# Reordering the detoured half of an exact attention: scores, fetches and GpSimd cuts of the long sequence

## The chip, the cores and the metric

The kernel runs on one core of one Trainium2 chip. The metric is the device time of one execution in microseconds (us), as a median over runs. Each core has TensorE (PE; its weight loads are shown as PEld), VectorE (DVE), ScalarE (ACT), GpSimd (POOL) and SyncE (SP), which here only issues DMAs. Each engine works through its own list of instructions in order, and they wait for each other with semaphores.

## The reference

One encoder layer over two sequences, x_prompt with 1024 tokens and x_sample with 512, width 1024, all in float32. Branch A is grouped-query attention: 8 query heads, 2 key/value groups of 4 heads each, head size 64, normalised and rotated q and k.

```python
def block(qi):
    s = jnp.einsum('bqkgd,bskd->bkgqs', qi, k, preferred_element_type=jnp.float32) * scale
    p = jax.nn.softmax(s, axis=-1)
    return jnp.einsum('bkgqs,bskd->bqkgd', p.astype(v.dtype), v)
...
merged = jax.nn.sigmoid(ga) * (o_a @ w_proj_a) + jax.nn.sigmoid(gb) * (o_b @ w_proj_b)
return merged @ w_out
...
h = h + _token_mixer(_rmsnorm(h, norm_mix_g[l]), ...)
hn = _rmsnorm(h, norm_mlp_g[l])
h = h + jnp.square(jax.nn.relu(hn @ w_mlp_up[l])) @ w_mlp_down[l]
```

Branch B (neighbourhood attention), the gates and the two-layer MLP are computed as well; the change does not touch them.

## The kernel before

Matrix products keep float32 precision by splitting each operand into a high part (rounded to fp32r by ScalarE) and a low part (value minus high part, by VectorE or GpSimd), and multiplying the parts separately. The kernel takes the short sequence first, then the long one, then the MLP. For each sequence and each of the two groups g there is a projection stage and then an attention stage, phase `phA`. In the profile the attention stages of the long sequence (NB == 2) lie at about 445 to 575 us (g = 0) and 640 to 765 us (g = 1).

An attention stage of the long sequence has eight units (h, qb): head h of the group, 512 queries (qb = 0 or 1), 1024 keys. A unit's scores are four tiles of 128 queries, one `step_s(u, j)` each:

- `s_tile` (L801 to L814): four score matmuls into a PSUM tile ss of 1024 columns (there are two such tiles); VectorE takes the maximum (nms, L804); ScalarE takes the exponential into an SBUF tile ps (L811; there are eight such buffers, tag "P"); VectorE takes the reciprocal of the sum (rls, L813); GpSimd multiplies by it (L814).
- For qb = 1, `turn_a` (L856, L857) follows at the next `step_s`: VectorE transposes the tile in blocks of 32 x 32 and SyncE writes it to DRAM (tas).

The value product needs the probabilities with keys on partitions. The two halves get there differently.

- *Transposed unit*, qb = 0: `t_chunk` (L838 to L842) transposes a chunk of 128 keys on TensorE (pTs); ScalarE makes the high part pths, VectorE the low part ptls.
- *Detoured unit*, qb = 1: `fetch_a` (L882) reads a quarter back from DRAM, 512 KB with the block order changed, into hqs. The first three quarters take slots of a shared pool of eleven; three are to be had, so a fetch for the next head needs the slot of the same quarter of this one to have been read. The fourth quarter takes two of the eight ps buffers. `cut_a` splits a quarter: ScalarE writes the high part (L887), GpSimd subtracts in place (L888, one instruction of 128x1024).

`pv` (L825, L826) multiplies a chunk's high and low part with the values, two matmuls into os; `next_pv` runs two chunks behind. A chunk of a detoured unit reads half of each of a quarter's 16 blocks of 64 columns: `(t[:, :, kc % 2 * 32 : kc % 2 * 32 + 32] for t in quarter[...])`. Between these, `fill.pull` puts matmuls of branch A's gate (gpss, L214), whose weights are loaded and split too (w_gs, L201 on ScalarE and L208 on VectorE).

After the first eight score tiles, of (0,1) and (0,0), each head h runs two loops of eight steps kc: in the first the transposed unit's chunks are transposed, in the second the detoured unit's chunks are queued. The order in which this is written is a priority: a planner at build time writes each engine's list by it and by its own estimate of when operands and buffers are ready, so neighbouring pieces can change places.

Of the kernel before, what the change touches and what calls it, by code (L numbers as in the profile page):

```python
# [11 lines left out]
F32 = mybir.dt.float32  # L12
# [3 lines left out]
ALU = mybir.AluOpType  # L16
# [45 lines left out]
def encoder(ctx: ExitStack, tc: tile.TileContext, xs, outs, w):  # L62
    nc = tc.nc
# [359 lines left out]
    def run(tr, nxt, first):  # L423
# [9 lines left out]
        fill = Fill()  # L433
# [105 lines left out]
        for g in range(2):  # L539
            with phase(f"phR{N}_{g}") as ph:  # L540
# [175 lines left out]
                for tt in range(NT):  # L716
# [19 lines left out]
                    op = nc.sync.dma_start(rt, w["rope"][tt * P : (tt + 1) * P])  # L736
# [52 lines left out]
            with phase(f"phA{N}_{g}") as ph:  # L789
# [55 lines left out]
                def next_pv():  # L845
                    if len(queue) > LAG:
                        pv(*queue.pop(0))
# [11 lines left out]
                def step_s(u, j):  # L859
                    end = s_tile(u, j)  # L860
                    while due:
                        turn_a(*due.pop(0))
                    if u[1]:
                        due.append((u, j))
                    return end
# [3 lines left out]
                def fetch_a(u, i):  # L869
                    nm = f"{N}_{g}_{u[0]}_{i}"  # L870
                    if i < 3:
                        hl = slot([P, 2, 16, 64], F32R, f"hq{nm}")
                        hi, lo = hl[:, 0], hl[:, 1]
                    else:
                        hi, lo = (
                            ph.tile([P, T], F32, tag="P", name=f"hq{nm}_{e}", bufs=8)
                            .bitcast(F32R)
                            .rearrange("p (a w) -> p a w", w=64)
                            for e in range(2)
                        )  # L880
                    src = PD[u].rearrange("t (a i) (b w) -> i b (t a) w", i=32, b=4)[:, :, :, 64 * i : 64 * i + 64]
                    nc.sync.dma_start(lo.bitcast(F32), src)  # L882
                    quarter[u, i] = hi, lo

                def cut_a(u, i):
                    hi, lo = quarter[u, i]
                    nc.scalar.activation(hi, lo.bitcast(F32), AF.Copy)  # L887
                    nc.gpsimd.tensor_tensor(lo, lo.bitcast(F32), hi.bitcast(F32), op=ALU.subtract)  # L888

                if NB == 2:  # L890
                    for u in ((0, 1), (0, 0)):
                        for j in range(4):
                            last_exp[:] = [step_s(u, j)]
                            fill.pull(1)
                    for h in range(4):
                        for kc in range(NT):
                            t_chunk((h, 0), kc)
                            if h < 3 and kc in (1, 4):
                                step_s((h + 1, 1), kc // 4)
                            if kc < 4:  # L900
                                fetch_a((h, 1), kc)
                            if 3 <= kc < 6:
                                cut_a((h, 1), kc - 3)
                            fill.pull(1 if kc % 4 < 3 else 0)
                            next_pv()
                        for kc in range(NT):
                            if kc == 1:
                                cut_a((h, 1), 3)
                            if h < 3 and kc < 6:
                                step_s(*(((h + 1, 1), 2 + kc // 3) if kc % 3 == 0 else ((h + 1, 0), kc - 1 - kc // 3)))  # L910
                            hi, lo = (t[:, :, kc % 2 * 32 : kc % 2 * 32 + 32] for t in quarter[(h, 1), kc // 2])
                            queue.append(((h, 1), kc, hi, lo))
                            fill.pull(0 if kc in (2, 5) else 1)
                            next_pv()
                else:
                    for j in range(4):
                        ends = s_tile(units[0], j)
                        last_exp[:] = [ends]
                        fill.pull(2)
                    for ui, u in enumerate(units):  # L920
                        h, qb = u
                        if first:
                            bias_row(g * 4 + ui)
                            if g == 0 and ui == 1:
                                early["a"] = load_a(1)
                            if g == 0 and ui == 2:
                                early["v"] = load_v(1, slot)
                        nxt_u = units[ui + 1] if ui + 1 < len(units) else None
                        sdone = 0
                        for kc in range(NT):  # L930
                            t_chunk(u, kc)
                            if nxt_u is not None:
                                while sdone < 4 and kc >= (0, 0, 1, 2)[sdone]:
                                    s_tile(nxt_u, sdone)
                                    sdone += 1

                            fill.pull(1)
                            next_pv()
# [1146 lines left out]
```

## Time and profile before

| what | value |
|---|---|
| median of 3 runs | 2114.34 us (2113.94 to 2116.36) |
| profiled execution, its own time | 2112.54 us |
| its span, first to last instruction | 2110.7 us |
| TensorE busy | 2072.8 us, 98% |
| VectorE, ScalarE, GpSimd busy | 1491.8, 1143.9, 441.1 us |
| mean granted TensorE clock | 0.999 |

The rows of a timeline give start, length, engine, line, operation, output <- inputs, shape and count; in brackets stands how long the engine stood idle before and what ended that. Rows of a group give busy time and the mean length in ns, then the idle time before them. Rows of a source line give minimum, median and maximum length in ns, then first and last start. Rows of waits give total, number and longest in us.

### The profile page before, as it was taken

How to read it: one execution, taken by the hardware profiler on the slowest of the kernel's cores; microseconds unless marked ns; L12 is line 12 of the kernel's file. 1: busy time of each engine (PE TensorE's matmuls, PEld its weight loads, DVE VectorE, ACT ScalarE, POOL GpSimd, SP SyncE). 2: the span in 40 equal slices, each digit the busy share in tenths (PEclk: the TensorE clock that was granted, in tenths of full speed). 3: DMA queues.
4: the chain of work that ended last, by engine and by line, in shares of the span. 5: the costliest groups of instructions: out<-in, count | busy, mean ns of one | idle time of the engine just before them, and what ended most of it. 6: DMA issues, size and time to landing. Idle time of an engine off the chain costs nothing.

```text
span 2110.7 us, 31228 instructions
## 1 busy us (share of the span) xinstructions
PE 2072.8 (98%) x10615; PEld 1808.7 (86%) x10615; DVE 1491.8 (71%) x2761; ACT 1143.9 (54%) x2455; POOL 441.1 (21%) x478
## 2 busy tenths in 40 slices
PE   9999999999999999999999999999999999999998
PEld 8887878986797778888888999999999988888887
DVE  6665886778658766778864877787777777669563
ACT  6664653766666655556522566565556634334442
POOL 2232310346535634543101100012000000000000
PEclk9999999999999999999999999999999999999999
DMA  6437557556635686776553565478444899688561
GB/s 193 135 103 209 160 162 254 179 134 173 168 82 153 184 197 197 236 237 210 177 197 135 190 200 192 157 242 222 148 156 150 285 346 343 210 277 280 161 209 61
DMA packets 406758, 406.45 MB, mean 193 GB/s; under 512 B 97599, under 2 KB 333767, under 8 KB 406599
## 3 DMA queue, kind: packets, MB, share of 16 engines
q1 hardware_dynamic: 368119, 339.16, 52.3%
q10 hardware_dynamic: 31328, 45.11, 6.4%
q0 software_dynamic: 7152, 20.19, 3.6%
q8 instruction: 84, 1.38, 0.3%
q14 instruction: 75, 0.61, 0.1%
HBM read 291.06 MB, written 114.10 MB: 192 GB/s over the span
## 4 chain that ended last, share of the span: by engine, by line
PE 69%; POOL 4%; issue 2%; DVE 2%; DMA 1%; ACT 1%; ACTq 0%; POOLq 0%; SPq 0%; DVEq 0%
PE dn L214 20%; PE ua L214 6%; PE ud L214 6%; PE uc L214 6%; PE gpss L214 5%; PE ops L214 4%; PE ub L214 3%; PE ppbs L214 2%; PE ppas L214 2%; PE pqbs L214 2%; PE pkbs L214 2%; PE zs L214 2%; POOL ps L814 2%; POOL hqs L888 2%; PE zvs L214 2%
## 5 line engine op out<-in xcount | busy, mean ns | idle before, releaser
L214 PE MATMUL dn<-wd,ah 128*128 128x512 f32 x1248 | 384.3, 389 | 0.0
L214 PEld LDWEIGHTS dn<-wd,ah 128*128 128x128 f32 x1248 | 234.2, 188 | 48.6
L214 PE MATMUL dn<-wd,al 128*128 128x512 f32 x624 | 242.8, 389 | 0.0
L1559 ACT ACTIVATE ah<-ar 128x512 fp32r<-128x512 f32 x168 | 104.0, 627 | 198.1 <-PE dn L214 184.9
L214 PE MATMUL gpss<-xs_0h,w_gs 128*128 128x512 f32 x512 | 185.8, 400 | 0.4 <-DVE w_gs L208 0.3
L1560 DVE TENSOR_TENSOR al<-ar,ah 128x512 fp32r<-128x512 f32 x168 | 113.9, 686 | 72.8 <-ACT ah L1559 63.0
L214 PE MATMUL ud<-B,A 128*128 128x384 f32 x768 | 143.6, 334 | 0.7 <-DVE c L1677 0.7
L214 PE MATMUL uc<-B,A 128*128 128x384 f32 x768 | 143.7, 334 | 0.0
L214 PE MATMUL ua<-B,A 128*128 128x384 f32 x768 | 138.8, 334 | 0.0
L214 PEld LDWEIGHTS dn<-wd,al 128*128 128x128 f32 x624 | 117.1, 188 | 24.4
L214 PEld LDWEIGHTS ud<-B,A 128*128 128x128 f32 x768 | 134.0, 188 | 1.1 <-DVE c L1677 1.1
L214 PEld LDWEIGHTS uc<-B,A 128*128 128x128 f32 x768 | 134.0, 188 | 0.2 <-ACT A L1559 0.2
L214 PEld LDWEIGHTS ua<-B,A 128*128 128x128 f32 x768 | 133.7, 188 | 0.2
L811 ACT ACTIVATE ps<-ss,nms 128x1024 f32<-128x1024 f32 (+1 forms) x96 | 93.5, 975 | 65.5 <-DVE nms L804 53.3
L180 POOL TENSOR_TENSOR rs_f<-ms_f,mhalf 128x1 f32<-128x1 f32 x6 | 4.0, 668 | 590.7 <-DVE ms_f L176 590.7
L814 POOL TENSOR_SCALAR ps<-ps,rls 128x1024 f32<-128x1024 f32 (+1 forms) x96 | 95.7, 999 | 129.9 <-DVE rls L813 113.9
L804 DVE TENSOR_REDUCE nms<-ss 128x1 f32<-128x1024 f32 (+1 forms) x96 | 99.3, 1037 | 30.1 <-PE ss L802 28.9
L214 PE MATMUL ops<-wh_os,mgs 128*128 128x512 f32 x384 | 119.5, 390 | 0.0
L214 PEld LDWEIGHTS gpss<-xs_0h,w_gs 128*128 128x128 f32 x512 | 96.1, 189 | 18.8 <-DVE w_gs L208 0.7
L214 PE MATMUL gpss<-xs_0l,w_gs 128*128 128x512 f32 x256 | 101.3, 396 | 0.0
L1559 ACT ACTIVATE A<-S 128x512 fp32r<-128x512 f32 x128 | 75.8, 623 | 31.5 <-DVE S L1622 22.7
L214 PE MATMUL gpss<-xs_1h,w_gs 128*128 128x512 f32 x256 | 90.2, 394 | 0.0
(299 smaller groups left out, 5169.8 us busy)
## 6 DMA issues: line engine op xcount, KB each, us to landing
ar<-ud SPq DMA_DIRECT2D x120, 512.0 KB, 4.7
br<-in_w_mlp_down_dram SPq DMA_DIRECT2D x72, 512.0 KB, 4.9
rawu<-in_w_mlp_up_dram SPq DMA_DIRECT2D x64, 512.0 KB, 4.1
ud<-c ACTq DMA_DIRECT2D x128, 192.0 KB, 3.3
raw_gs<-in_w_in_dram SPq DMA_DIRECT2D x32, 512.0 KB, 3.9
tas<-ps SPq DMA_DIRECT2D x32, 512.0 KB, 2.8
hqs<-tas SPq DMA_DIRECT2D x32, 512.0 KB, 7.0
ud<-cs SPq DMA_DIRECT2D x64, 192.0 KB
```

The source lines that it names most:

```text
L180: op = nc.gpsimd.tensor_tensor(r[:, :n], m[:, :n], mhalf[:, :n], op=ALU.pow)
L214: op = nc.tensor.matmul(out, a, b, **kw)
L804: nc.vector.tensor_reduce(nm_, s, axis=AX.X, op=ALU.max, negate=True)
L811: op = nc.scalar.activation(to, of, AF.Exp, bias=nm_, accum_out=l)
L814: nc.gpsimd.tensor_scalar(p, p, rl, 1.0, op0=ALU.mult, op1=ALU.mult)
L888: nc.gpsimd.tensor_tensor(lo, lo.bitcast(F32), hi.bitcast(F32), op=ALU.subtract)
L1559: nc.scalar.activation(hi, src, AF.Copy)
L1560: nc.vector.tensor_tensor(lo, src, hi.bitcast(F32), op=ALU.subtract)
```

## The change

Only branch A of the long sequence is touched.

- The subtract of `cut_a` becomes two instructions, over blocks 0 to 7 and 8 to 15.
- The first three fetches of unit (0,1) stand ahead of the first head's loops. For later heads, quarters 0 and 1 are fetched in steps 4 and 6 of the second loop of the head before, quarter 2 in step 0 and quarter 3 in step 2 of the head's own first loop. (Before: quarters 0 to 3 in steps 0 to 3.)
- The cuts stand in steps 1, 2 and 5 of the first loop and step 0 of the second. (Before: 3, 4, 5 and 1.)
- Detoured scores: all four tiles of (1,1) stand in the first head's first loop; those of (h+2,1) are spread over steps 5 and 7 of head h's second loop and steps 1 and 4 of head h+1's first loop. (Before: (h+1,1) in steps 1 and 4 of head h's first loop and steps 0 and 3 of its second.)
- Transposed scores of (h+1,0) stand in steps 0, 1, 2 and 4 of the second loop (before: 1, 2, 4 and 5). In the second loop the steps that pull no gate matmuls are 1 and 4 (before: 2 and 5).

```diff
                 def cut_a(u, i):
                     hi, lo = quarter[u, i]
                     nc.scalar.activation(hi, lo.bitcast(F32), AF.Copy)
-                    nc.gpsimd.tensor_tensor(lo, lo.bitcast(F32), hi.bitcast(F32), op=ALU.subtract)
+                    for a in (slice(0, 8), slice(8, 16)):
+                        nc.gpsimd.tensor_tensor(lo[:, a], lo[:, a].bitcast(F32), hi[:, a].bitcast(F32), op=ALU.subtract)
...
+                    for i in range(3):
+                        fetch_a((0, 1), i)
                     for h in range(4):
+                        u, nn, nd = (h, 1), (h + 1, 0), (h + 1, 1)
                         for kc in range(NT):
                             t_chunk((h, 0), kc)
-                            if h < 3 and kc in (1, 4):
-                                step_s((h + 1, 1), kc // 4)
-                            if kc < 4:
-                                fetch_a((h, 1), kc)
-                            if 3 <= kc < 6:
-                                cut_a((h, 1), kc - 3)
+                            if h == 0 and kc in (0, 2, 4, 6):
+                                step_s(nd, kc // 2)
+                            elif 0 < h < 3 and kc in (1, 4):
+                                step_s(nd, 2 + kc // 4)
+                            if kc == 0 and h > 0:
+                                fetch_a(u, 2)
+                            if kc == 2:
+                                fetch_a(u, 3)
+                            if kc in (1, 2, 5):
+                                cut_a(u, kc // 2)
                             fill.pull(1 if kc % 4 < 3 else 0)
                             next_pv()
                         for kc in range(NT):
-                            if kc == 1:
-                                cut_a((h, 1), 3)
-                            if h < 3 and kc < 6:
-                                step_s(*(((h + 1, 1), 2 + kc // 3) if kc % 3 == 0 else ((h + 1, 0), kc - 1 - kc // 3)))
-                            hi, lo = (t[:, :, kc % 2 * 32 : kc % 2 * 32 + 32] for t in quarter[(h, 1), kc // 2])
-                            queue.append(((h, 1), kc, hi, lo))
-                            fill.pull(0 if kc in (2, 5) else 1)
+                            if kc == 0:
+                                cut_a(u, 3)
+                            if h < 3 and kc in (0, 1, 2, 4):
+                                step_s(nn, min(kc, 3))
+                            if h < 2 and kc in (5, 7):
+                                step_s((h + 2, 1), kc // 7)
+                            hi, lo = (t[:, :, kc % 2 * 32 : kc % 2 * 32 + 32] for t in quarter[u, kc // 2])
+                            queue.append((u, kc, hi, lo))
+                            fill.pull(0 if kc in (1, 4) else 1)
                             next_pv()
+                            if h < 3 and kc in (4, 6):
+                                fetch_a(nd, kc // 2 - 2)
```

## The prediction

> **What bounds the kernel now.** I read, in this order: the page's busy shares, the sums by stage, the waits of TensorE in each stage, and the timelines around the longest waits. "Stage 1" and "stage 2" are the two attention stages of the long sequence, one for each key/value group: the only place that the diff touches.
>
> ```profile
> span 2110.7 us, 31228 instructions
> PE 2072.8 (98%) x10615; PEld 1808.7 (86%) x10615; DVE 1491.8 (71%) x2761; ACT 1143.9 (54%) x2455; POOL 441.1 (21%) x478
> ```
>
> The sums by stage (columns: length, then busy time of PE, PEld, DVE, ACT, POOL, then the granted clock):
>
> ```profile
> 445.00:580.00 135.00, 125.85 (x600) 97.92 (x599) 101.36 (x135) 87.47 (x143) 75.42 (x48) 1.00 0.65 169
> 640.00:775.00 135.00, 125.67 (x594) 97.43 (x593) 98.00 (x135) 84.80 (x134) 74.42 (x49) 1.00 0.69 183
> ```
>
> TensorE is the bound: it idles 2110.7 - 2072.8 = 37.9 us in all, and 135 - 125.85 = 9.15 us in stage 1 and 135 - 125.67 = 9.33 us in stage 2, at a granted clock of 1.00 in both. The diff changes neither the number nor the shape of TensorE's instructions, so its gain lies inside these 18.5 us. The waits of stage 1 (in total, times, longest):
>
> ```profile
> PE os L826 <- POOL hqs L888: 4.0, 4, 1.7
> PE pTs L838 <- POOL ps L814: 2.6, 5, 0.9
> PE os L826 <- DVE ptls L842: 1.2, 2, 0.9
> PE os L825 <- DVE ptls L842: 0.4, 1, 0.4
> ```
>
> And of stage 2:
>
> ```profile
> PE os L826 <- POOL hqs L888: 3.5, 2, 1.8
> PE pTs L838 <- POOL ps L814: 2.6, 5, 0.9
> PE pTs L838 <- DVE ptls L842: 1.7, 1, 1.7
> ```
>
> Three kinds: the value product of a detoured unit waits for GpSimd's subtract of a cut (7.5 us in both stages), the transposes of a transposed unit wait for GpSimd's normalisation (5.2), and both wait for VectorE's low halves ptls (1.2 + 0.4 + 1.7).
>
> **The change, part by part.**
>
> *Fetches and cuts earlier (term 1).* Now all four score tiles of a detoured unit are turned and written before any of its fetches may start, and its last score stands half a head before its first fetch. The last unit of stage 1 shows the consequence (SyncE's four fetches; GpSimd's first cut; TensorE's waits; the row of 755.33 is stage 2's):
>
> ```profile
> 553.34 7.00 SPq L882 DMA_DIRECT2D hqs<-tas  x4
> 560.36 2.37 POOL L888 TENSOR_TENSOR hqs<-hqs 128x1024 fp32r<-128x1024 f32 x1 [8.28 <-ACT hqs L887]
> 562.78 0.50 PE L826 MATMUL os<-hqs,vhls 128*128 128x512 f32 x1 [1.10 <-POOL hqs L888]
> 566.19 0.50 PE L826 MATMUL os<-hqs,vhls 128*128 128x512 f32 x1 [0.33 <-POOL hqs L888]
> 574.38 0.50 PE L826 MATMUL os<-hqs,vhls 128*128 128x512 f32 x1 [0.88 <-POOL hqs L888]
> 755.33 0.50 PE L826 MATMUL os<-hqs,vhls 128*128 128x512 f32 x1 [1.79 <-POOL hqs L888]
> ```
>
> The fetches run from 553.3 to 560.3, the first cut is subtracted at 560.4 after GpSimd stood idle 8.28 us, and TensorE, with nothing else left, waits 1.10 + 0.33 + 0.88 = 2.31 us; stage 2's last unit costs 1.79 us. After the change the last unit's scores end in the first loop of the head before, its first two fetches are issued in that head's second loop as slots are read, the third at the start and the fourth in the third step of its own head. Its data should lie in SBUF some 10 us sooner, against a lateness of 2 us: these 4.1 us go. In the middle of the stage, VectorE first:
>
> ```profile
> 503.92 3.54 DVE L208 TENSOR_TENSOR w_gs<-raw_gs,w_gs 128x512 fp32r<-128x512 f32 x2
> 507.38 0.21 DVE L813 RECIPROCAL rls<-ls 128x1 f32<-128x1 f32 x2
> ```
>
> GpSimd and TensorE beside it, and the same wait in stage 2:
>
> ```profile
> 503.90 2.40 POOL L888 TENSOR_TENSOR hqs<-hqs 128x1024 fp32r<-128x1024 f32 x1 [0.93 <-ACT hqs L887]
> 507.70 2.23 POOL L814 TENSOR_SCALAR ps<-ps,rls 128x1024 f32<-128x1024 f32 x2 [1.40 <-DVE rls L813]
> 509.90 2.35 POOL L888 TENSOR_TENSOR hqs<-hqs 128x1024 fp32r<-128x1024 f32 x1
> 514.59 2.23 POOL L814 TENSOR_SCALAR ps<-ps,rls 128x1024 f32<-128x1024 f32 x2
> 512.30 0.50 PE L826 MATMUL os<-hqs,vhls 128*128 128x512 f32 x1 [1.73 <-POOL hqs L888]
> 515.76 0.33 PE L838 MATMUL pTs<-ident,ps 128*128 128x128 f32 x1 [0.61 <-POOL ps L814]
> 704.22 0.51 PE L826 MATMUL os<-hqs,vhls 128*128 128x512 f32 x1 [1.73 <-POOL hqs L888]
> ```
>
> The third cut (509.90) stands behind two normalisations that wait for VectorE's reciprocal at 507.38, and ends at 512.25, when TensorE has waited 1.73 us; the row of 704.22 is stage 2's, the same 1.73. In the new order the first two cuts stand in the second and third step of the head and the third in the sixth, ahead of the second loop's scores. Sum of the term: 4.1 + 3.46 = 7.56, the 7.5 of the two wait rows. Bounds: 0 (data or cuts are as late as now) and 7.5. I take 7.5, since the fetches move by much more than TensorE waits.
>
> *Next transposed unit's scores first (term 2).* The wait of 0.61 at 515.76 ends with a normalisation that ran only at 514.59, right after the cuts. Its like in the next head:
>
> ```profile
> 544.68 0.33 PE L838 MATMUL pTs<-ident,ps 128*128 128x128 f32 x1 [0.85 <-POOL ps L814]
> ```
>
> Together 1.46, and as the rows of both stages show the same 2.6 in five such waits, 2.9 for both. The third cut now leaves that place, the fourth stays just ahead of these scores: I take half, 1.5, with bounds 0 and 2.9.
>
> *Subtract by halves (term 3).* Of the split's two instructions no matmul can start after one: a value product reads all 16 blocks, and the halves divide these. What changes is how long GpSimd keeps others out. VectorE's subtract of a gate weight took 503.92 to 506.85 beside the cut of 503.90, against 0.67 where it met none:
>
> ```profile
> L208 DVE TENSOR_TENSOR w_gs<-raw_gs,w_gs x4: 669/1483/2934, 472.4 to 506.8; 128x512 fp32r<-128x512 f32 x4
> 473.61 2.29 DVE L208 TENSOR_TENSOR w_gs<-raw_gs,w_gs 128x512 fp32r<-128x512 f32 x1
> 476.62 0.50 PE L826 MATMUL os<-ptls,vhls 128*128 128x512 f32 x1 [0.93 <-DVE ptls L842]
> L368 POOL TENSOR_TENSOR B<-ta,B x12: 1286/1300/1312, 1151.0 to 1437.9; 128x512 fp32r<-128x512 f32 x12
> L888 POOL TENSOR_TENSOR hqs<-hqs x12: 2353/2402/2958, 469.5 to 566.7; 128x1024 fp32r<-128x1024 f32 x12
> ```
>
> Such a block (2.29, where 0.67 is its own) held the ptls that TensorE waited 0.93 us for; stage 2's like is the 1.7. A half should last as a 128x512 subtract of GpSimd does, 1.30: the longest block falls by 2.40 - 1.30 = 1.1, and the two waits from 0.93 + 1.7 to about 0.6. Gain 2.0, bounds 0 (VectorE has to wait for both halves) and 2.6. The price is 2 x 1.30 - 2.40 = 0.2 us a cut, 3.2 us a stage on GpSimd, which has 135 - 75.4 = 59.6 us free: nothing, as long as the cuts are early; if they were still last, 0.2 on each of the six waits, 1.2.
>
> [...]
>
> *First head heavier (term 4, a cost).* All four scores of unit (1,1) now stand in the first head's first loop, two before. One costs VectorE a maximum, a reciprocal and a turn:
>
> ```profile
> L804 DVE TENSOR_REDUCE nms<-ss 128x1 f32<-128x1024 f32 x32 | 38.8, 1213 | 12.6 <-PE ss L802 12.5
> L813 DVE RECIPROCAL rls<-ls 128x1 f32<-128x1 f32 x32 | 4.7, 150 | 2.5 <-ACT ps L811 2.3
> L856 DVE STREAM_TRANSPOSE ps<-ps 128x1024 f32<-128x1024 f32 x16 | 19.7, 1233 | 2.8 <-POOL ps L814 2.7
> 466.00:483.00 17.00, 16.07 (x81) 12.50 (x80) 15.38 (x21) 13.54 (x22) 13.52 (x8) 1.00 0.94 210
> 480.70 1.25 DVE L856 STREAM_TRANSPOSE ps<-ps 128x1024 f32<-128x1024 f32 x1 [0.45 <-POOL ps L814]
> ```
>
> That is 1.21 + 0.15 + 1.23 = 2.6 us, and two of them 5.2. VectorE has 17 - 15.38 = 1.6 free there. But the third turn runs at 480.70 already, so about one comes forward: 2.6 - 1.6 = 1.0 a stage, 2.0 in all; bounds 0 and 10.4. Buffers are short there too: of eight score tiles (0,0) holds four and the fourth fetch, one step earlier than now, two, which leaves two for the four tiles of (1,1); a score without one waits in PSUM, and its price is within the same 10.4.
>
> *Fetches blocked (term 5, a cost).* A fetch into a slot that is still read holds SyncE, and behind it stand turned tiles' writes and gate weights; ScalarE, in order too, stands when it reaches a cut whose data is not there. The 16 fetches a stage stay 7.00 / 4 = 1.75 us of SyncE each. On GpSimd a cut moved forward now stands ahead of normalisations, but they can be placed between its halves, so it holds them 1.30 instead of 2.40.
>
> ```profile
> DMA to landing us min/median/max: 4.2/7.0/8.1
> ACT hqs L887 <- DMA hqs<-tas: 3.0, 5, 1.3
> ```
>
> Stage 2 shows 3.0 us of it on ScalarE, which works 84.8 of 135 us. TensorE has gate matmuls to put in; I take 1.0 in all. Bounds 0 and the price of rival (c).
>
> **Sum.** -7.5 - 1.5 - 2.0 + 2.0 + 1.0 = -8.0 us. The profiled execution took 2112.54 us (span 2110.7 and 1.8 around it), 1.8 under the median 2114.34; it would take 2104.5, and the median 2106.3, -0.38%.
>
> **Rivals.**
>
> (a) The waits only move. The order on each engine is written afresh by the planner, and its misjudged times give new waits of the old size; in the first head VectorE is short by the full 5.2 us a stage. Then 10.4 takes the place of 2.0 in term 4: +0.4, 2114.7; if only the last units' 4.1 go, 2110.2. For it: VectorE's 15.38 of 17. Against it: at the end of a stage no score is left, so the 4.1 have nothing to turn into.
>
> (b) More goes: terms 1 to 3 at their upper bounds and no cost, 7.5 + 2.9 + 3.3 (all ptls waits shown, 1.2 + 0.4 + 1.7) = 13.7, 2100.6.
>
> (c) ScalarE stands at the cuts. Twelve cuts of sixteen stand in first loops, beside the transposes' high halves, and now nearer the head's start; in the first head the first two stand 2 and 3 steps behind their fetches instead of 4. If each of the 24 is reached x us before its data and TensorE pays all of it, the sum is -11 + 2 + 24x; slower than the bound of 0.2% from x = 0.55, about the 3.0 / 5 = 0.6 of the row above. At x = 0.8, within the 8.1 - 7.0 by which the slowest landing exceeds the median, it is +10.2, 2124.5. Against it: a cut is planned where its data is expected, and now 1 of 16 waits in stage 1.
>
> (d) VectorE goes between the halves and the cuts end later: 1.30 + 0.67 + 1.30 = 3.27 for 2.40. If the cuts are still last at the six waits, term 1 is +6 x 0.87 = +5.2 and the sum +4.7, 2119.0. Against it: the earlier fetches of term 1 would have to fail first. [...]
>
> **Chances.** Forecast 0.53, (b) 0.07, (a) 0.27, (c) 0.10, (d) 0.03. Two medians of this kernel under 0.2% (4.2 us) apart can hardly be told from no change. Faster: forecast and (b), 0.60; same: (a), 0.27; slower: (c) and (d), 0.13. The range runs from (b)'s 2100.6, rounded down to 2100, to 2117.0, a little past (a)'s worse value; the forecast alone lies in 2101 to 2110.
>
> **What would show it.** Right: no waits for hqs at the end of either stage, with the last cut well before TensorE's last value product; the L208 subtracts under 2 us; idle time of TensorE in the two stages near 5 us each; everything after stage 2 shifted by 8 us and otherwise alike. Wrong: waits for ptls or for turned scores in the first head (a), ScalarE waiting for hqs landings with the transposed halves behind it (c), or stages before and after these two changing in length, which nothing here provides for.

## The result and the profile after

The changed kernel takes 2105.72 us (median of 7 runs, 2104.78 to 2108.55); the kernel before took 2115.63 us beside it (7 runs, 2113.85 to 2117.34). The ratio is 0.9957, with a 95% interval of 0.9945 to 0.9968: faster by 0.43%. The forecast was 2106.3 us, a ratio of 0.9962 on the median then known.

The profiled execution after took 2105.40 us (span 2103.6), the one before 2112.54 us. So the profiles show 7.1 us of the 9.9 between the medians; the last experiment asks about the rest. The page after, span and busy shares:

```profile
span 2103.6 us, 31314 instructions
PE 2072.8 (99%) x10615; PEld 1809.0 (86%) x10615; DVE 1477.5 (70%) x2761; ACT 1142.2 (54%) x2455; POOL 445.6 (21%) x510
```

TensorE's work is the same 2072.8 us to the tenth; what fell is its idle time, from 37.9 to 2103.6 - 2072.8 = 30.8 us. The sums of the two attention stages (columns as before; each window has moved with the work, and the first ends 5 us sooner because the stage does):

```profile
445.00:575.00 130.00, 124.08 (x593) 96.92 (x592) 98.05 (x137) 87.49 (x147) 78.20 (x64) 1.00 0.68 177
635.00:770.00 135.00, 130.62 (x614) 101.08 (x613) 93.82 (x140) 87.05 (x139) 81.83 (x69) 1.00 0.72 190
```

TensorE now idles 130 - 124.08 = 5.9 us in stage 1 (9.15 before) and 135 - 130.62 = 4.4 us in stage 2 (9.33 before): 10.3 instead of 18.5. TensorE's waits in stage 1 after (total, times, longest):

```profile
PE pTs L838 <- DVE ptls L842: 2.9, 3, 1.4
PE pTs L838 <- POOL ps L814: 1.0, 3, 0.4
PE ss L801 <- ACT ps L811: 0.8, 1, 0.8
PE os L826 <- DVE ptls L842: 0.6, 2, 0.4
```

And in stage 2:

```profile
PE pTs L838 <- DVE ptls L842: 1.5, 2, 0.7
PE pTs L838 <- POOL ps L814: 1.0, 3, 0.4
PE ss L801 <- ACT ps L811: 0.8, 1, 0.8
PE os L826 <- DVE ptls L842: 0.8, 3, 0.4
```

The row that led both lists before, the value product waiting for a cut (hqs), is gone: 7.5 us to nothing. The waits for normalised scores (ps) fell from 2.6 to 1.0 in each stage. The waits for the low halves (ptls) did not fall; they rose from 3.9 us before (the 1.2 + 0.4 + 1.7 shown and 0.4 + 0.2 more in stage 2) to 2.9 + 0.6 + 1.5 + 0.8 = 5.8 us. One instruction behind stage 2 shows the shift of all that follows, first in the timeline before, then in the one after:

```profile
787.82 0.44 PE L214 MATMUL sbs<-kBs,qBs 128*128 128x384 f32 x1 [0.48 <-DVE kBs L1120]
```

```profile
779.80 0.45 PE L214 MATMUL sbs<-kBs,qBs 128*128 128x384 f32 x1 [0.48 <-DVE kBs L1132]
```

It runs 8.02 us sooner with the same wait of 0.48 before it; 0.9 us of that is lost again behind it, where the change doesn't reach (the spans differ by 7.1).

### The profile page after: what moved, and what is told of

Read it like the earlier page. It is cut to its first block, busy times and chain, and to the rows that moved or that the text cites. A ratio compares the mean times of both kernels' runs of the same rounds, so it can differ in the third digit from the quotient of the medians.

```text
span 2103.6 us, 31314 instructions
## 1 busy us (share of the span) xinstructions
PE 2072.8 (99%) x10615; PEld 1809.0 (86%) x10615; DVE 1477.5 (70%) x2761; ACT 1142.2 (54%) x2455; POOL 445.6 (21%) x510
## 3 DMA queue, kind: packets, MB, share of 16 engines
q8 instruction: 84, 1.38, 0.3%
```

## The experiments

Four parts of the change can be taken apart: the subtract by halves, the places of the fetches and cuts, the places of the detoured units' scores (their *lead*), and the transposed units' scores first in their loop. Theory F is the one of the prediction's first term as its heading has it: earlier fetches and cuts removed the hqs waits, and the halves shortened the ptls waits. Theory D says that the lead did it: a fetch can't start before the last turned tile of its unit has been written, so places of fetches mean little without it. A third point is the clock. Each time is told against the kernel before on the same chip.

### The halves alone, and the change without them

On the kernel before:

```diff
-                    nc.gpsimd.tensor_tensor(lo, lo.bitcast(F32), hi.bitcast(F32), op=ALU.subtract)
+                    for a in (slice(0, 8), slice(8, 16)):
+                        nc.gpsimd.tensor_tensor(lo[:, a], lo[:, a].bitcast(F32), hi[:, a].bitcast(F32), op=ALU.subtract)
```

Expected:

> The kernel before with the subtract in two halves and nothing else. TensorE's idle time in the two stages was 18.5 us before and is 10.3 after the whole change. My theory (terms add; halves are term 3): only the two waits behind a blocked VectorE subtract go, idle about 16.5 us, time 2 us under before; the waits for hqs stay near 7.5. [...] Second rival (halves cost, term 1's bound): cuts end 0.2 us later, idle 19 to 20, time 1 us over before. Under both, gate-weight subtracts last at most about 1.5 us where they lasted 2.9.

And the changed kernel with the same lines put back to the whole subtract. Expected:

> The changed kernel with the subtract as one instruction again. My theory: only the blocked VectorE comes back; waits for hqs stay at 0 because the cuts are early; idle 10.3 + 2 = about 12.5, time 2 us over the changed kernel. [...] Second rival (halves are pure overhead once the cuts are early): idle 10, time equal.

Measured: the halves alone 2116.34 us against 2115.67 before, ratio 1.0004 (0.9995 to 1.0013); the change without them 2106.06, ratio 0.9956 (0.9944 to 0.9969), beside the 0.9957 of the whole change. The first kernel's source line of the gate-weight subtract and its waits for cuts and low halves in stage 1 (the cut is line 889 there):

```profile
L208 DVE TENSOR_TENSOR w_gs<-raw_gs,w_gs x4: 680/1482/1815, 474.9 to 508.1; 128x512 fp32r<-128x512 f32 x4
```

```profile
PE os L826 <- POOL hqs L889: 4.7, 5, 1.9
PE os L826 <- DVE ptls L842: 1.1, 2, 0.9
```

The mechanism is there: the longest gate-weight subtract falls from 2934 to 1815 ns, as 1.1 us was predicted. But the ptls wait of 0.9 stays, and the hqs wait grows from 4.0 to 4.7. In stage 2 the ptls wait of 1.7 does shrink, to 0.5; TensorE idles 18.0 us in both stages instead of 18.5, where 16.5 was expected, and no run's time shows it. In this profile a stretch of 3.41 us at half clock (see below) takes half of that, 1.7 us, as well, so the halves alone do not price themselves. The other run tells more: without the halves the changed kernel idles 9.1 us in the two stages where it idles 10.3 with them, and its gate-weight subtracts in stage 1 are just as short (source line of the changed kernel, then of the one with the whole subtract):

```profile
L208 DVE TENSOR_TENSOR w_gs<-raw_gs,w_gs x4: 666/677/1403, 478.0 to 516.9; 128x512 fp32r<-128x512 f32 x4
L208 DVE TENSOR_TENSOR w_gs<-raw_gs,w_gs x4: 665/676/1406, 477.7 to 516.4; 128x512 fp32r<-128x512 f32 x4
```

So the new order shortens them, not the halves. No gain of the halves is seen here, with or without the rest of the change.

### The scores put back, the fetches put back

The changed kernel with both kinds of scores, and the steps that pull no gate matmuls, at their old places (fetches, cuts and halves stay):

```diff
-                            if h == 0 and kc in (0, 2, 4, 6):
-                                step_s(nd, kc // 2)
-                            elif 0 < h < 3 and kc in (1, 4):
-                                step_s(nd, 2 + kc // 4)
+                            if h < 3 and kc in (1, 4):
+                                step_s(nd, kc // 4)
...
-                            if h < 3 and kc in (0, 1, 2, 4):
-                                step_s(nn, min(kc, 3))
-                            if h < 2 and kc in (5, 7):
-                                step_s((h + 2, 1), kc // 7)
+                            if h < 3 and kc < 6:
+                                step_s(*((nd, 2 + kc // 3) if kc % 3 == 0 else (nn, kc - 1 - kc // 3)))
...
-                            fill.pull(0 if kc in (1, 4) else 1)
+                            fill.pull(0 if kc in (2, 5) else 1)
```

Expected:

> The changed kernel with all scores (and the steps without gate matmuls) where they stood before; fetches, cuts and halves stay moved. My theory: a fetch cannot start before its unit's last score tile is turned and written, so the first fetches of a head start only some 2 to 4 us sooner than before instead of some 10, and the last unit's waits for hqs come back in part (2 of 4.1 us); with term 2's 1.5 lost as well, idle about 13.5 to 14, time 3 to 4 us over the changed kernel. Rival (places of fetches and cuts alone do it): no hqs waits, idle about 10 to 11, time equal to the changed kernel.

The changed kernel with fetches and cuts at their old places (scores and halves stay):

```diff
-                    for i in range(3):
-                        fetch_a((0, 1), i)
...
-                            if kc == 0 and h > 0:
-                                fetch_a(u, 2)
-                            if kc == 2:
-                                fetch_a(u, 3)
-                            if kc in (1, 2, 5):
-                                cut_a(u, kc // 2)
+                            if kc < 4:
+                                fetch_a(u, kc)
+                            if 3 <= kc < 6:
+                                cut_a(u, kc - 3)
...
-                            if kc == 0:
+                            if kc == 1:
                                 cut_a(u, 3)
...
-                            if h < 3 and kc in (4, 6):
-                                fetch_a(nd, kc // 2 - 2)
```

Expected:

> The changed kernel with fetches and cuts where they stood before; scores and halves stay moved. My theory: fetches issue at the head's start at once, since the data has long been written, but land about 7 us later and the four cuts take 4 x 2.6 us of GpSimd: at the end of a stage about half of the 4.1 us of hqs waits return, idle about 12.5 to 13, time 2 to 3 us over the changed kernel. Rival (the scores alone do it): no hqs waits, idle about 10 to 11, time equal. Second rival (fetches alone do it): all 7.5 us of hqs waits return, idle 17.

Measured: old scores 2127.67 us, ratio 1.0054 (1.0042 to 1.0067), slower than before; old fetches 2107.18, ratio 0.9963 (0.9949 to 0.9976), nearly the whole gain. Stage 1's waits with old scores, and SyncE's timeline for the last unit there:

```profile
PE pTs L838 <- POOL ps L814: 3.3, 5, 1.1
PE os L826 <- DVE ptls L842: 2.5, 3, 1.3
PE ss L801 <- ACT ps L811: 2.5, 4, 0.8
PE os L826 <- POOL hqs L889: 1.9, 2, 1.5
```

```profile
535.04 22.51 SPq L857 DMA_DIRECT2D tas<-ps  x4
560.09 3.92 SPq L882 DMA_DIRECT2D hqs<-tas  x3
```

The first two of these fetches are written a loop earlier than before, and yet they run at 560.09, behind four writes of turned tiles that take until 557.55 (535.04 + 22.51). In the kernel before it was the same pair of rows, the fetches of 553.34 quoted in the prediction and ahead of them these writes, to 531.26 + 19.75 = 551.0:

```profile
531.26 19.75 SPq L857 DMA_DIRECT2D tas<-ps  x4
```

With the old fetches and the new scores SyncE's fetches of this unit stand at:

```profile
537.89 9.23 SPq L882 DMA_DIRECT2D hqs<-tas  x4
```

15 us sooner than before, though their lines are where they were. Theory F falls for the first term: moved fetches and cuts with the old scores lose 12 us, the scores without them keep all but about 1.5, with 0.5 us of waits for hqs in each stage. The 12 us by which old scores are slower are explained in part. Their five executions run from 2122.77 us at a mean clock of 0.999 to 2129.30 at 0.995, and the profile is of the last. In it TensorE's idle time in the two stages is 22.7 us instead of 18.5, and two windows of 6.83 us each run at half clock; by the matmuls counted in such a window (below: 9 in 3.40 us, 17 in the 3.40 behind it) that costs about half their length, 6.8 us. TensorE's busy time is 11.3 us more than before (2084.1 to 2072.8); the 4.5 us beyond those 6.8 are not explained.

### The lead alone

On the kernel before, only the detoured scores at their new places:

```diff
-                            if h < 3 and kc in (1, 4):
-                                step_s((h + 1, 1), kc // 4)
+                            if h == 0 and kc in (0, 2, 4, 6):
+                                step_s((1, 1), kc // 2)
+                            elif 0 < h < 3 and kc in (1, 4):
+                                step_s((h + 1, 1), 2 + kc // 4)
...
-                            if h < 3 and kc < 6:
-                                step_s(*(((h + 1, 1), 2 + kc // 3) if kc % 3 == 0 else ((h + 1, 0), kc - 1 - kc // 3)))
+                            if h < 3 and kc in (1, 2, 4, 5):
+                                step_s((h + 1, 0), kc - 1 - kc // 3)
+                            if h < 2 and kc in (5, 7):
+                                step_s((h + 2, 1), kc // 7)
```

Expected:

> The kernel before with one thing of the change alone: the detoured units' scores at their new, earlier places. The subtracts stay whole, the fetches, the cuts and the transposed units' scores stay where they were. Theory D (the lead of the detoured scores is the cause): 5 to 7 us under the kernel before, TensorE's idle time in the attention stage about 12 to 13 us instead of 18.5, the waits for hqs under 1.5 us together instead of 7.5. Rival (the lead works only together with the transposed units' scores being first in their heads): within 2.5 us of the kernel before, the waits for hqs gone but the waits for the scores' banks (ps) and for ScalarE longer by as much.

The changed kernel ran on the same chip again. Expected:

> The changed kernel once more, unaltered, on the chip of the two runs beside it, so that they can be compared head to head: 2105 to 2107 us, 0.995 to 0.997 of the kernel before.

Measured: the lead alone 2106.99 us, ratio 0.9959 (0.9947 to 0.9972); the changed kernel 2105.85, ratio 0.9955 (0.9942 to 0.9967), both against 2115.28. The one edit brings 8.3 of 9.4 us, more than theory D's 5 to 7; as the intervals overlap, it is not shown that the rest of the change adds to it. The longer waits in stage 1 with the lead alone, and SyncE's timeline of the last unit:

```profile
PE pTs L838 <- POOL ps L814: 2.9, 3, 2.5
PE os L826 <- DVE ptls L842: 1.4, 2, 1.0
PE pTs L838 <- DVE ptls L842: 1.2, 2, 0.7
```

```profile
534.09 0.33 SPq L857 DMA_DIRECT2D tas<-ps  x1
537.27 8.74 SPq L882 DMA_DIRECT2D hqs<-tas  x4
```

No wait for hqs is left in stage 1, nor in stage 2. The last turned tile is written at 534.09 instead of about 551, and fetches whose lines did not move run 16 us sooner. In the middle of the stage the third cut, which ended at 512.25 before, ends at 508.1 (GpSimd's second and third cut there):

```profile
503.31 4.78 POOL L888 TENSOR_TENSOR hqs<-hqs 128x1024 fp32r<-128x1024 f32 x2
```

TensorE's idle time in both stages is 11.7 us (theory D: 12 to 13). The rival is wrong on the time; of its waits, ps grew to 2.9 in stage 1 (2.6 before) and fell to 1.9 in stage 2, so only the longest one, 2.5 us, looks like it.

### The transposed scores first, alone and undone

On the kernel before, with the halves, the loop of the transposed units changed alone:

```diff
-                            if h < 3 and kc < 6:
-                                step_s(*(((h + 1, 1), 2 + kc // 3) if kc % 3 == 0 else ((h + 1, 0), kc - 1 - kc // 3)))
+                            if h < 3 and kc in (0, 3):
+                                step_s(nd, 2 + kc // 3)
+                            if h < 3 and kc in (0, 1, 2, 4):
+                                step_s(nn, min(kc, 3))
...
-                            fill.pull(0 if kc in (2, 5) else 1)
+                            fill.pull(0 if kc in (1, 4) else 1)
```

Expected:

> The kernel before with halves (worth nothing by e1 and e2) and the next transposed unit's scores, and the steps without gate matmuls, at their new places; detoured scores, fetches and cuts as before. e4 showed that the places of the scores bring nearly all of the gain. Theory D (the detoured scores half a head ahead bring it): waits for hqs stay near 7.5 us, idle time in the two stages 16 to 18 us, time within 2 us of before. Rival (earlier transposed scores bring it, by clearing the second loop's end): the waits for turned scores go from 5.2 to under 2.5 and idle to about 13, time 4 to 5 us under before.

And the changed kernel with the transposed scores back in steps 1, 2, 4 and 5 and the pulls with them:

```diff
-                            if h < 3 and kc in (0, 1, 2, 4):
-                                step_s(nn, min(kc, 3))
+                            if h < 3 and kc in (1, 2, 4, 5):
+                                step_s(nn, kc - 1 - kc // 3)
...
-                            fill.pull(0 if kc in (1, 4) else 1)
+                            fill.pull(0 if kc in (2, 5) else 1)
```

Expected:

> The changed kernel with the transposed unit's scores, and the steps without gate matmuls, back at their old places. Theory D: only the waits for turned scores grow, by my term 2 of 1.5 us, idle about 12, time 1 to 2 us over the changed kernel. Rival (as in e5): idle 15 or more, time 5 us over.

Measured: alone 2113.67 against 2115.77, ratio 0.9990 (0.9981 to 0.9999), its hqs waits 3.9 + 1.8 us (theory D: near 7.5) and its ps waits 3.3 + 3.3, more than the 2.6 + 2.6 before; undone 2108.84, ratio 0.9970 (0.9958 to 0.9982). The undone kernel's longest waits in stage 1:

```profile
PE pTs L838 <- POOL ps L814: 3.3, 3, 2.6
```

So this part is worth about 2 us alone (0.2 to 4.0 by its interval) and about 3 in the change. Without it ps is waited for 2.6 us in one piece (at 548.71), the very wait of 2.5 that the lead alone has too, and in that profile a window of 3.41 us at half clock stands beside it, 1.7 us of the 3. But the parts do not add up: the lead alone, at 0.9959, lacks this part too and is no slower than the undone kernel, which has the moved fetches, cuts and halves besides. The intervals of the lead alone, of the undone and of the changed kernel overlap, so the price of this part inside the change is not shown closer.

### The last head's subtracts on VectorE

What is left in stage 1 after the change is longest in the last head (a ptls wait of 1.4). Whole subtract, and for unit (3,1) on the other engine, with one gate pull moved from the last loop to the first scores:

```diff
+                    eng = nc.vector if u[0] == 3 else nc.gpsimd
+                    eng.tensor_tensor(lo, lo.bitcast(F32), hi.bitcast(F32), op=ALU.subtract)
...
-                            fill.pull(1)
+                            fill.pull(2 if (u[1], j) == (0, 1) else 1)
...
-                            fill.pull(0 if kc in (1, 4) else 1)
+                            fill.pull(0 if kc in (1, 4) or (h, kc) == (3, 6) else 1)
```

Expected:

> A version meant to beat the changed kernel: whole subtracts, the last head's four on VectorE (which has no scores left then), one gate step moved from the last loop to before the first head, where TensorE waits 0.84 us for a score tile in PSUM. If the reading of the waits is right: the 1.0 us wait for ptls at the last head of stage 1 and both waits of 0.84 go, idle from 9.6 (e2) to about 7, time 2 to 3 us under the changed kernel. Rival: VectorE's subtract of a 128x1024 cut (some 1.4 us) comes between the last head's ptls, and these waits take the place of the others: idle 9 to 10, time equal.

And again beside the changed kernel on one chip. Expected:

> The version with the whole subtract and the last head's four subtracts on VectorE again, beside the changed kernel on one chip. Theory (the waits for the last head's ptls, 1.0 and 1.4 us, were on the path): 1 to 2 us under the changed kernel. Rival (the first time was a favourable chip): equal within 0.5 us.

Measured: 2104.06 us, ratio 0.9946 (0.9934 to 0.9959), then 2105.14, ratio 0.9953 (0.9939 to 0.9966), beside the changed kernel's 2105.85. The subtract takes half the time on VectorE (source line of the first run, both engines):

```profile
L889 POOL TENSOR_TENSOR hqs<-hqs x18: 2370/2401/2426, 469.6 to 714.8; 128x1024 fp32r<-128x1024 f32 x18
L889 DVE TENSOR_TENSOR hqs<-hqs x6: 1206/1225/1516, 544.6 to 736.7; 128x1024 fp32r<-128x1024 f32 x6
```

The last head's waits for ptls went as meant. The two waits of 0.84 us for a score tile, which the moved gate pull was to end, stayed (0.82 and 0.83), and the waits for the scores' PSUM banks (ss) grew from 0.8 to 2.2 in all in each stage. Head to head it is 0.7 us, inside both intervals: it is not shown to be faster than the changed kernel, and the rival of the second run (equal within 0.5 us) is nearer than the theory.

### When the clock halves

Three of these profiles (old scores, halves alone, transposed scores undone) show TensorE at half clock within a stage, which the kernel before did not. The old-scores kernel's timeline and the window around it:

```profile
557.29 0.55 PE L838 MATMUL pTs<-ident,ps 128*128 128x128 f32 x3 [1.10 <-POOL ps L814]
558.66 0.90 PE L838 MATMUL pTs<-ident,ps 128*128 128x128 f32 x3 [0.82 <-POOL ps L814]
```

```profile
556.30:559.80 3.50, 1.45 (x6) 0.81 (x6) 1.03 (x3) 2.02 (x5) 2.06 (x2) 0.81 0.50 199
```

Two waits, neither of them over 1.10 us, left TensorE 1.45 us busy in 3.5; after them the records show 0.5 of the clock for 6.83 us. The kernel with the halves alone shows it after one wait of 1.86 us (timeline, then two windows: up to its end and behind it):

```profile
514.87 0.50 PE L826 MATMUL os<-hqs,vhls 128*128 128x512 f32 x1 [1.86 <-POOL hqs L889]
```

```profile
511.40:514.90 3.50, 1.64 (x8) 0.97 (x7) 3.50 (x4) 1.04 (x2) 3.50 (x4) 1.00 0.72 239
515.40:518.80 3.40, 3.40 (x9) 2.67 (x9) 1.00 (x2) 1.21 (x2) 2.99 (x3) 0.50 0.76 190
```

Nine matmuls run in the window at 0.50, and 17 in the 3.40 us behind it. To measure it by itself, waits of several lengths were put into TensorE's list in the last MLP stage of the kernel before, each a number n of copies by ScalarE that the next transpose needs:

```diff
+        def wait_pe(n):
+            tc.keep_in_program_order(nc.tensor.transpose(probe[:, 0:P], ident, ident))
+            for _ in range(n):
+                tc.keep_in_program_order(nc.scalar.activation(pt_, probe, AF.Copy))
+            tc.keep_in_program_order(nc.tensor.transpose(probe[:, P : 2 * P], pt_[:, 0:P], ident))
...
+            if i >= 16 and i % 6 == 3:
+                wait_pe((i // 6) % 6)
```

Expected:

> Not about the change's parts but about a side effect seen in e1 and e3: stretches of 3.41 and 6.83 us at half the granted clock, right after waits. The kernel before, with waits put into the last matrix stage of the MLP: at every sixth block of twelve matmuls a small transpose waits for n copies of 128x512 on ScalarE (n = 0 to 5 in turn, some 0.6 us each), with TensorE's other work held behind it; an extra PSUM bank is taken and nothing of the result is changed. [...] Second rival (the halving in e1 and e3 had another cause): no wait halves it. Time: the sum of the waits, about 45 us over before, and 1.7 us for each halved window.

Measured (one execution): 2207.27 us, mean clock 0.986. That is 91.5 us over the kernel before: the waits sum to 57.3 us instead of the 45 expected, and the half-clock stretches of 58 us in all cost half of that, 29. Three waits in its timeline, and a window behind each, in the same order:

```profile
2083.70 0.33 PE L1988 MATMUL probe<-ident,probe_s 128*128 128x128 f32 x1 [1.73 <-ACT probe_s L1987]
1862.11 0.33 PE L1988 MATMUL probe<-ident,probe_s 128*128 128x128 f32 x1 [2.35 <-ACT probe_s L1987]
1981.12 0.33 PE L1988 MATMUL probe<-ident,probe_s 128*128 128x128 f32 x1 [2.35 <-ACT probe_s L1987]
```

```profile
2083.70:2087.70 4.00, 4.00 (x18) 3.33 (x19) 0.69 (x1) 0.63 (x1) 0.00 (x0) 1.00 0.00 0
1863.30:1866.50 3.20, 3.20 (x9) 2.52 (x8) 0.17 (x1) 0.00 (x0) 0.00 (x0) 0.50 0.85 270
1981.20:1984.60 3.40, 3.40 (x16) 2.80 (x17) 2.38 (x4) 0.34 (x1) 0.00 (x0) 1.00 0.82 243
```

The three waits of 1.73 us never halved the clock, one of the two of 2.35 did, all of 2.58 us and longer did, for 3.41 or 6.83 us. The rival that no wait halves it falls. In the attention stages it is as uneven: the wait of 2.60 us with the transposed scores undone has a half-clock window beside it, the one of 2.50 with the lead alone has none. What sets these apart is not shown. For the changed kernel this weighs little. The most idle time in any 3.41 us of the stages was 1.79 us before and is 1.38 us after, and neither profiled execution has a half-clock window there.

### The kernel before, once more

Unaltered, one execution. Expected:

> The kernel before once more, unaltered, for a second profiled execution of it: the first took 2112.54 us, 3.1 us less than the median of the runs beside the changed kernel, so that the two profiles show 7.1 of 9.9 us. Theory (the longest waits for hqs, 1.7 to 1.8 us, lie just under what halves the clock, and some executions cross it): the second profile is longer by 1 to 4 us, shows a window of 3.41 us at half clock in an attention stage, and TensorE's busy time is up by as much. Rival (the executions differ by small amounts everywhere): no such window, the idle time and busy time of every stage within a few tenths. If it takes 2112 to 2113 us again, nothing is told apart.

Measured: 2116.44 us, span 2114.4, 3.7 us longer than the first profile. The sums of the two stages:

```profile
445.00:580.00 135.00, 125.79 (x598) 97.64 (x597) 101.01 (x136) 86.14 (x136) 75.30 (x48) 1.00 0.66 171
640.00:775.00 135.00, 125.42 (x591) 96.89 (x590) 99.00 (x137) 85.32 (x135) 74.47 (x49) 1.00 0.67 179
```

The theory falls: the clock is 1.00 in both stages and the waits for hqs are 4.1 and 3.7 us (4.0 and 3.5 in the first profile). The stages idle 9.2 + 9.6 = 18.8 us, as before; the 3.7 us lie elsewhere, such as a wait of 1.20 us for xs_1l at 402.60, ahead of the stages, which was 0.51 in the first profile. (A wait for hqs of 1.93 us here did not halve the clock.) So executions of one kernel differ by some us outside the changed stages, and the first profile was a short one. The changed kernel's second profile (span 2104.0) idles 5.9 + 4.5 = 10.4 us in the stages, much as its first did. This second pair of spans differs by 10.4 us, and 8.4 of it is idle time of the stages (18.8 less 10.4). The 8 us of the two stages are the change's; the 1.9 us by which the medians differ more are not seen in any pair of profiles at one place.

## Why the prediction was right, and where its steps were not

**Total.** Forecast 2106.3, measured 2105.72; forecast -8.0 us in the two stages, measured 10.3 - 18.5 = -8.2, and the shift of 8.02 behind stage 2. The signs to look for came: no hqs waits, gate-weight subtracts under 2 us (1.40 at most), idle time near 5 us a stage (5.9 and 4.4), all else shifted by 8. That it comes out to a few tenths is luck in part. The ps waits fell by 1.7 us more than forecast, and the ptls waits rose by 1.9 where terms 3 and 4 together had them unchanged. Terms 2, 3 and 5 are wrong in size, term 1 has its gain under the wrong name, and term 4 gives the wrong reason; the errors cancel.

**Term 1, fetches and cuts earlier, -7.5.** The size is right: 4.0 + 3.5 us to nothing. The working named the cause in passing (all four scores of a unit are turned and written before its fetches may start) but booked it under fetches and cuts. The runs separate them: scores 16 us sooner bring fetches 16 us sooner by themselves (lead alone, -8.3 us), while moved fetches and cuts without the lead are slower than before. With the fetches and cuts put back, 1.0 of the 7.5 us of hqs waits returns. "The fetches move by much more than TensorE waits" was right about the result, through the scores. The last cut of stage 1 after the change, in GpSimd's timeline:

```profile
554.71 2.71 POOL L889 TENSOR_TENSOR hqs<-hqs,hqs 128x512 fp32r<-128x512 f32 x2
```

It ends at 557.4; the last wait for a cut before was at 574.38.

**Term 2, transposed scores first, -1.5.** Under-sized. The ps waits fell from 2.6 to 1.0 in each stage, -3.2 us, where half of 2.9 had been taken. Undone, they return (3.3 and 2.4) and 3 us with them, though with an interval that also holds the 1.5. Without the lead the working is not borne out: alone, with the halves, this part let the ps waits rise to 3.3 in each stage.

**Term 3, halves, -2.0.** This step failed. Alone the halves made the longest block shorter as predicted, but "and the two waits from 0.93 + 1.7 to about 0.6" did not follow: they changed no run's time, left out of the change they are not missed, and the ptls waits rose by about 2 us. The lower bound of 0 had stood for "VectorE has to wait for both halves"; it came out for another reason. In the new order the gate weights' subtracts of the first head stand behind the ptls (478.00 in the changed kernel) and two of them take 1.27 us, with halves or without, so there is no block to shorten; ahead of the ptls stands a turn, as the next term shows. That VectorE gets in after the first half was the author's estimate; what the runs show is the length of the longest gate-weight subtract in stage 1, 2934 ns with whole subtracts and 1815 with the halves alone, where the shortest take 669 and 680.

**Term 4, first head heavier, +2.0.** There are waits of about this size, but not for the reason given, and not as a cost on top. VectorE's timeline in the first head after, and TensorE's waits beside it:

```profile
474.46 1.25 DVE L856 STREAM_TRANSPOSE ps<-ps 128x1024 f32<-128x1024 f32 x1 [1.37 <-POOL ps L814]
475.63 1.25 DVE L842 TENSOR_TENSOR ptls<-pTs,pths 128x512 fp32r<-128x512 f32 x2
```

```profile
476.34 0.66 PE L838 MATMUL pTs<-ident,ps 128*128 128x128 f32 x4 [0.73 <-DVE ptls L842]
482.15 0.50 PE L826 MATMUL os<-ptls,vhls 128*128 128x512 f32 x1 [0.41 <-DVE ptls L842]
```

A turn (line 856) that itself waited for its normalisation stands ahead of the ptls: 0.73 + 0.41 = 1.14 us in stage 1, and the same in stage 2 (0.73 + 0.40), 2.3 in all. The reason given was that VectorE has 1.0 us too little time in each first head. But it stands idle for 1.37 us just ahead of that turn, because GpSimd runs the normalisation only behind a cut (halves from 470.76, the normalisation at 473.29).

The lead alone tells whether it is a cost. It has the heavier first head and the whole subtracts, so terms 3 and 4, added, would give it the 2.6 us of before and 2.0 more. TensorE's waits there:

```profile
477.54 0.66 PE L838 MATMUL pTs<-ident,ps 128*128 128x128 f32 x4 [0.60 <-DVE ptls L842]
483.35 0.50 PE L826 MATMUL os<-ptls,vhls 128*128 128x512 f32 x1 [0.42 <-DVE ptls L842]
```

With 0.58 + 0.42 in stage 2 that is 2.0 in all, less than the 0.93 + 1.66 before. The new order takes a blocked subtract from ahead of the ptls and puts a waiting turn there: one exchange, which the prediction had booked as a gain of the halves and a cost of the scores. Its sum is near nothing, as forecast; neither term has its size.

The other 3.5 us of ptls waits lie in later heads. Two of 0.7 us stand behind such a turn again, and the 1.4 in the last head of stage 1 stands behind weight subtracts (two of 128x256 take 2.84 us from 554.86) beside the cut of 554.71, halves and all. No step of the prediction had those, and only the last head's was tried (subtracts on VectorE), with no gain that can be told.

**Term 5, fetches blocked, +1.0.** Not found; it went the other way. No fetch held TensorE, and SyncE spends less time on one (source line of the fetches, before and after):

```profile
L882 SPq DMA_DIRECT2D hqs<-tas x32: 370/1774/4214, 464.1 to 751.5; - x32
```

```profile
L882 SPq DMA_DIRECT2D hqs<-tas x32: 359/427/3622, 463.5 to 729.2; - x32
```

The "1.75 us of SyncE each" of the working was no price of a fetch but of four in a row: spread out, the median is 0.43. Rival (c) had no ground: ScalarE waits 0.9 us for landings of fetches in the whole span, 3.2 before. Rival (d) shows in the last head of stage 1, without its price: two halves from 551.38 take 3.36 us beside a weight's subtract on VectorE (1.78 us from 551.81), but no wait for a cut follows; the halves' median is 1.29 us, the predicted 1.30. Rival (a) has a part in it, the 2 us of ptls waits.

The sum by waits is then -7.5 (hqs) - 3.2 (ps) + 1.9 (ptls, 3.9 to 5.8 with the waits of 0.4 and 0.2 in stage 2 that the prediction did not show) + 0.8 (small waits for rls and ot_As in place of others) = -8.0.

## What to carry to other kernels

When a consumer waits at the end of a chain (score, turn, write, fetch, cut, product), find the link that can't start, not the one that is seen waiting: moving the fetches and cuts without the scores made this kernel slower, moving the scores brought the fetches along without touching them. A shorter block of one engine by another (here 2934 to 1815 ns, and no run's time changed) is worth something only if what then runs first is what the bound engine waits for; look at what stands next in that engine's list. And test the parts of a change singly and left out: here one of four edits carried 8.3 of 9.4 us, and two terms of a sum that came out right were one exchange.

## What the runs showed of the hardware

The records show TensorE at half clock after some of its waits, and no single length of wait decides it. In the attention stages one wait of 1.86 us (halves alone), or 1.10 and 0.82 close together (old scores), was enough for 3.41 and 6.83 us at half clock, while one of 1.93 us (the kernel before, second profile) was not. Among the waits put into the last MLP stage three of 1.73 us were not enough, one of two of 2.35 us was, and all of 2.58 us and longer were. In the profile with the halves alone 9 matmuls ran in 3.40 us at half clock and 17 in the 3.40 us behind it. From these numbers I estimate that a new wait of 2 us can cost nearly twice its length where TensorE is the bound: half of 3.41, 1.7 us, on top.
